# The z columns of the first two sequence tiles, computed row block by row block

## The chip, the cores and the metric

The kernel runs on one core of a Trainium2 chip. A core has TensorE (PE, matrix multiplies), VectorE (DVE), ScalarE (ACT), GpSimd (POOL) and SyncE (SP, which issues most transfers). Each engine works through its own list of instructions in order; semaphores hold an instruction until what it needs is there. The metric is the device time of one execution in microseconds, the median of several runs.

## The reference

One encoder layer: an RMS norm, one projection W_in, attention and a state-space branch on its columns, gates, and an output projection.

```python
h = _rms_norm(x, pre_norm_g[l])
z = h @ w_in[l]
z_q, z_kv, z_kr, g_attn, u_ssm, g_ssm = jnp.split(z, split_points, axis=-1)
attn = _mla_attention(z_q, z_kv, z_kr, positions, ...)
ssm = _s5_bidirectional(u_ssm, ...)
...
x = x + _rms_norm(mixed, post_norm_g[l])
```

x is 2048 x 1024, W_in is 1024 x 1984. The change touches only `h @ w_in`, and of it only the first 448 columns (z_q, z_kv and z_kr, which the kernel calls z) of the first two of 16 sequence tiles.

## The kernel before, in words

The first phase computes h @ W_in. The sequence is cut into 16 tiles of 128 positions, which are taken in pairs. A tile is loaded (`load_x`), scaled by its norm (`norm_x`: squares and their sum on ScalarE, a power on GpSimd, the scaling on VectorE), and turned (`turn`: eight 128x128 transposes on TensorE into PSUM).

Everything is multiplied in three passes, to keep float32 accuracy in a faster number format: an operand is split into a high part, which ScalarE writes, and the rest, which VectorE writes (`split`, lines 194 to 200). hh and hl are the parts of the turned x; wh and wl those of a block of weights. `mm3` (lines 202 to 205) issues the three matmuls high x high, high x low, low x high.

W_in's columns come as four blocks: z (448 columns), u, ga and gs (512 each). Each is loaded and split in 8 row blocks of 128 rows (`load_raw`, `split_w`, `load_w`), once, and stays in SBUF. `gemm` makes the z columns of one tile by 8 times 3 matmuls; `gemm_t` makes 256 columns of u or a gate for a pair of tiles, by 2 groups of 8 times 3 matmuls. `do_z` copies z out of PSUM on ScalarE, takes the squares of its two parts there, lets GpSimd scale them, and stores them. `do_u` and `do_gate` do the like.

The order on each engine is the order in which the program issues the instructions; no scheduler moves them. For the first pair that is: load x0 (in two halves), the first four row blocks of z's weights and x1; scale x0; split blocks 0 and 1; turn x0; split blocks 2, 3 and 4; scale x1; split blocks 5 to 7. Then the generator `blocks` (line 563) gives one step at a time: `do_z` of tile 0, with `turn` of tile 1 put in before its row block 5; then the split of u's weights (`load_w(*BLK[1])`); `do_z` of tile 1; then ga's split, the first half of u, gs's split, the second half, and the four gate steps. From the second pair on the weights are there and only x is loaded.

The raw row blocks lie in two rings: 7 buffers (`s5t`), and 8 (`stg`) for every fourth block; a load waits until its buffer is free. PSUM has 5 buffers for results (`psZ`), 2 for transposes and one (`psK`) that is used much later. Behind the first phase come attention with the state-space branch beside it, and the output projection.

Of the kernel before, what the change touches and what calls it, by code (L numbers as in the profile page):

```python
# [12 lines left out]
F32 = mybir.dt.float32  # L13
# [9 lines left out]
P = 128  # L23
SEQ = 2048
DM = 1024
KD = DM // P
NT = SEQ // P
# [4 lines left out]
NZ = 448  # L32
# [116 lines left out]
def tile_hymba(ctx, tc, x, pos, inv_freq, pre_g, w_in, q_g, w_uqT, w_uqr, kv_g, w_ukT, w_uv, attn_g,  # L149
# [4 lines left out]
    V, A, G, PE, SP = nc.vector, nc.scalar, nc.gpsimd, nc.tensor, nc.sync  # L154
# [14 lines left out]
    ident = con.tile([P, P], F32, tag="ident", name="ident")  # L169
# [9 lines left out]
    def small_consts():  # L179
        SP.dma_start(kvg, kv_g)  # L180
        V.tensor_scalar(kvgs, kvg, SCALE, None, ALU.mult)
        SP.dma_start(qg, q_g)
        V.tensor_scalar(qgs, qg, SCALE, None, ALU.mult)
# [9 lines left out]
    def split(hi, lo, src, scale=None):  # L193

        if scale is None:
            A.activation(hi, src, AF.Copy)
            V.tensor_tensor(lo, src, f32(hi), ALU.subtract)
        else:
            A.activation(hi, src, AF.Copy, scale=scale)
            V.scalar_tensor_tensor(lo, src, scale, f32(hi), ALU.mult, ALU.subtract)  # L200

    def mm3(ps, ahi, alo, bhi, blo, first, last):
        PE.matmul(ps, ahi, bhi, start=first, stop=False)  # L203
        PE.matmul(ps, ahi, blo, start=False, stop=False)  # L204
        PE.matmul(ps, alo, bhi, start=False, stop=last)  # L205
# [16 lines left out]
    def pool(st, name, bufs, **kw):  # L222
        return st.enter_context(tc.tile_pool(name=name, bufs=bufs, reuse_waits="tile", **kw))
# [5 lines left out]
    hh = hp.tile([P, KD, 2, P], F32R, tag="hh", name="hh")  # L229
    hl = hp.tile([P, KD, 2, P], F32R, tag="hl", name="hl")  # L230
# [6 lines left out]
    psZ = pool(ph1, "psZ", 5, space=PSUM)  # L237
    psK = pool(ph1, "psK", 1, space=PSUM)

    BLK = [("z", 0, NZ), ("u", 960, 512), ("ga", 448, 512), ("gs", 1472, 512)]  # L240
    wh, wl = {}, {}

    def load_raw(nm, c0, n, k):
        ring, tag = (stg, "st") if k % 4 == 3 else (s5t, "sc")
        raw = ring.tile([P, 512], F32, tag=tag, name=f"raw_{nm}{k}")
        SP.dma_start(raw[:, :n], w_in[k * P:(k + 1) * P, c0:c0 + n])
        return raw

    def split_w(nm, n, k, raw):
        if nm not in wh:  # L250
            wh[nm] = wp[nm].tile([P, KD, n], F32R, tag=f"wh_{nm}", name=f"wh_{nm}")
            wl[nm] = wp[nm].tile([P, KD, n], F32R, tag=f"wl_{nm}", name=f"wl_{nm}")
        split(wh[nm][:, k, :], wl[nm][:, k, :], raw[:, :n], preg[:, k:k + 1])

    def load_w(nm, c0, n, ks=range(KD)):
        for k in ks:
            split_w(nm, n, k, load_raw(nm, c0, n, k))

    def load_x(s):
        xt = xp.tile([P, DM], F32, tag="xt", name=f"xt{s}")  # L260
        SP.dma_start(xt, xv[s])
        return xt

    def norm_x(xt):
        junk = jp.tile([P, DM], BF16, tag="junk", name="junk")
        ss = sm.tile([P, 1], F32, tag="ss", name="ss")
        A.activation(junk, xt, AF.Square, accum_out=ss)
        r = rsqrt_of(ss, 1, 1.0 / DM)
        V.tensor_scalar(xt, xt, r, None, ALU.mult)

    def turn(xt, t):

        pts = []
        for j in range(2):
            pt = psT.tile([P, 4, P], F32, tag="pt", name="pt")
            for k in range(4):
                PE.transpose(pt[:, k, :], xt[:, (4 * j + k) * P:(4 * j + k + 1) * P], ident)
            pts.append(pt)
        for j in range(2):
            split(hh[:, 4 * j:4 * j + 4, t, :], hl[:, 4 * j:4 * j + 4, t, :], pts[j])  # L280

    def gemm(nm, n, t, between=None):
        ps = psZ.tile([P, 512], F32, tag="z", name=f"z_{nm}")
        for k in range(KD):
            if k == 5 and between:
                between()
            mm3(ps[:, :n], hh[:, k, t, :], hl[:, k, t, :], wh[nm][:, k, :], wl[nm][:, k, :], k == 0, k == KD - 1)
        return ps

    def do_z(s, between=None):  # L290
        ps = gemm("z", NZ, s % 2, between)
        z = stg.tile([P, 512], F32, tag="st", name="zst")
        A.activation(z[:, :NZ], ps[:, :NZ], AF.Copy)
        junk = jp.tile([P, DM], BF16, tag="junk", name="junk")
        ss = sm.tile([P, 2], F32, tag="ss2", name="ss2")
        A.activation(junk[:, :256], z[:, 0:256], AF.Square, accum_out=ss[:, 0:1])
        A.activation(junk[:, 256:384], z[:, 256:384], AF.Square, accum_out=ss[:, 1:2])
        v = sm.tile([P, 2], F32, tag="rv2", name="rv")
        r = sm.tile([P, 2], F32, tag="rr2", name="rr")
        V.tensor_scalar(v[:, 0:1], ss[:, 0:1], 1.0 / 256, EPS, ALU.mult, ALU.add)  # L300
        V.tensor_scalar(v[:, 1:2], ss[:, 1:2], 1.0 / 128, EPS, ALU.mult, ALU.add)
        G.tensor_tensor(r, v, nhalf[:, 0:2], ALU.pow)
        G.tensor_scalar(z[:, 0:256], z[:, 0:256], r[:, 0:1], None, ALU.mult)
        G.tensor_scalar(z[:, 256:384], z[:, 256:384], r[:, 1:2], None, ALU.mult)
        G.dma_start(z_d[s], z[:, :NZ])
# [256 lines left out]
    def step():  # L562

        VM.n -= BUDGET
        while VM.n < 0 and next(gen, "end") != "end":
            pass

    def blocks(s):


        pair = [(do_u, (s, 0)), (do_u, (s, 1)), (do_gate, (s, "ga", 0, 0)), (do_gate, (s, "ga", 1, 2)),
                (do_gate, (s, "gs", 0, 4)), (do_gate, (s, "gs", 1, 6))]
        x1 = xs[1]
        z0, z1 = [(do_z, (s, (lambda: turn(x1, 1)) if s <= 2 else None))], [(do_z, (s + 1,))]
        for f, a in z0 + z1 + pair if s in (0, NT - 2) else z0 + pair + z1:
            f(*a)
            yield

# [25 lines left out]
    xt = xp.tile([P, DM], F32, tag="xt", name="xt0")  # L604
# [1 line left out]
    for c in halves:  # L606
        SP.dma_start(xt[:, c], xv[0][:, c])
    SP.dma_start(preg, pre_g)
    raws = [load_raw(*BLK[0], k) for k in range(4)]
    xs = [xt, load_x(1)]  # L610
    ss = sm.tile([P, 2], F32, tag="ss2", name="ss")
    junk = jp.tile([P, DM], BF16, tag="junk", name="junk")
    for j, c in enumerate(halves):
# [3 lines left out]
    G.tensor_tensor(r, v, nhalf[:, :1], ALU.pow)  # L617
    for c in halves:
        V.tensor_scalar(xt[:, c], xt[:, c], r, math.sqrt(DM), ALU.mult, ALU.mult)
    for k in range(2):  # L620
        split_w("z", NZ, k, raws[k])
    turn(xt, 0)
    for k in range(2, 4):
        split_w("z", NZ, k, raws[k])
    load_w(*BLK[0], range(4, 5))
    norm_x(xs[1])
    load_w(*BLK[0], range(5, KD))
    for s in range(0, NT, 2):
        last = s + 2 == NT
        blk = blocks(s)  # L630
        for n in range(4 if last else 8):
            next(blk)
            if s == 0 and n == 0:
                load_w(*BLK[1])
                small_consts()
            if not last and n == 0:
                xs = [load_x(s + 2), load_x(s + 3)]
            if s == 0 and n in (1, 2):
                load_w(*BLK[1 + n])
            if not last and n in ((4, 5) if s == 0 else (1, 2)):  # L640
                norm_x(xs[n - (4 if s == 0 else 1)])
            if n == 7 and s == 0:
                turn(xs[0], 0)
            elif n >= 6 and s > 0:
                turn(xs[n - 6], n - 6)
            if s > 0:
                step()
# [895 lines left out]
    for t in range(8 * NU + LAG + AVLAG + 2):  # L1543
        n, i = divmod(t, 8)
# [44 lines left out]
        if n < NU and b + 1 < 8:  # L1589
            k = 8 * h + i  # L1590
# [70 lines left out]
def build(nc, arrays):  # L1661
    args = [nc.dram_tensor(f"in_{k}_dram", a.shape, mybir.dt.from_np(a.dtype), kind="ExternalInput").ap()
            for k, a in arrays.items()]
    outs = [nc.dram_tensor(f"out_{i}_dram", shape, mybir.dt.from_np(np.dtype(dtype)), kind="ExternalOutput").ap()
            for i, (shape, dtype) in enumerate(_OUTS)]
    with tile.TileContext(nc) as tc:
        tile_hymba(tc, *args, *outs)
# [11 lines left out]
```

## Time and profile before

| | us |
|---|---|
| median of 3 runs (lowest, highest) | 1382.09 (1381.69, 1382.13) |
| the profiled execution | 1382.02 |
| its span, first to last instruction | 1380.2 |
| TensorE busy | 1344.5 (97% of the span) |
| VectorE, ScalarE, GpSimd busy | 972.8, 796.5, 650.4 |

The profile gives, for each instruction, the engine, its start and how long it took. Busy time of TensorE counts overlapping matmuls once; the distance between the starts of two neighbours is its pace. A name such as `z_z<-wh_z,hh` says what is written and what is read. A row with a count (x8) is a run of like instructions, with the time from the first's start to the last's end.

### The profile page before, as it was taken

Reading aid. Unit: us, or ns where it says so; the run is one execution under the profiler, and the core shown is the slowest. Engines: PE = TensorE matmul, PEld = TensorE weight load, DVE = VectorE, ACT = ScalarE, POOL = GpSimd, SP = SyncE. Lnnn points to the kernel's source line nnn. Section 1 sums busy time; section 2 is a strip of 40 time slices with the busy share of each in tenths; the row PEclk is TensorE's granted clock in tenths of the full one; section 3 lists DMA queues with packets and bytes.
Section 4 is the critical chain, followed back from the end, with each engine's and each line's share of the span. In section 5 each row is a group of like instructions: output and inputs, shape, how many; then the busy total and the mean of one; then the engine's idle time right before and its main releaser. Section 6 shows DMA issues by size and latency. Waiting matters only on the chain.

```text
span 1380.2 us, 24302 instructions
## 1 busy us (share of the span) xinstructions
PE 1344.5 (97%) x9016; PEld 1216.5 (88%) x9016; DVE 972.8 (70%) x1812; ACT 796.5 (58%) x1828; POOL 650.4 (47%) x680
## 2 busy tenths in 40 slices
PE   7999999999989999999999999999999989999998
PEld 7999999999978888898888888888888778888886
DVE  6456564433288878888878879887887895867774
ACT  7312221222248778778777777777787775545542
POOL 2102311322447576575576666756641885333440
PEclk9999999999999999999999999999999999999999
DMA  8322323352630020201202011110101344455332
GB/s 300 89 54 72 88 69 78 87 130 62 147 90 23 9 67 9 51 24 28 47 5 63 13 35 41 27 41 9 30 9 35 100 130 111 146 174 168 124 107 92
DMA packets 122135, 102.93 MB, mean 75 GB/s; under 512 B 14672, under 2 KB 107104, under 8 KB 122016
## 3 DMA queue, kind: packets, MB, share of 16 engines
q1 hardware_dynamic: 110384, 89.43, 23.3%
q0 software_dynamic: 2272, 7.62, 2.2%
q10 hardware_dynamic: 9360, 4.33, 1.6%
q8 instruction: 70, 1.15, 0.4%
q14 instruction: 49, 0.40, 0.1%
HBM read 63.80 MB, written 37.54 MB: 73 GB/s over the span
## 4 chain that ended last, share of the span: by engine, by line
PE 79%; DVE 8%; POOL 5%; issue 3%; ACT 3%; DMA 2%; SPq 1%; POOLq 0%; DVEq 0%; ACTq 0%
PE pt L1151 5%; PE po L203 4%; PE po L204 4%; PE po L205 4%; PE sc L1103 3%; PE sc L1104 3%; PE sc L1107 3%; PE sc L1106 3%; PE av L1172 3%; PE av L1171 3%; PE av L1173 3%; PE sc L1105 3%; PE z_ga L204 2%; PE z_ga L205 2%; PE z_ga L203 2%
## 5 line engine op out<-in xcount | busy, mean ns | idle before, releaser
L1575 DVE TENSOR_TENSOR plo<-pt,phi 128x512 fp32r<-128x512 f32 x255 | 175.4, 688 | 58.0 <-ACT phi L1159 53.6
L1114 ACT ACTIVATE e<-sc,nm 128x512 f32<-128x512 f32 x256 | 175.8, 687 | 69.6 <-DVE nm L1108 69.0
L1108 DVE TENSOR_REDUCE nm<-sc 128x1 f32<-128x512 f32 x256 | 174.3, 681 | 49.1 <-PE sc L1107 47.7
L1159 ACT ACTIVATE phi<-pt 128x512 fp32r<-128x512 f32 x256 | 152.7, 596 | 75.3 <-PE pt L1151 74.2
L1143 ACT ACTIVATE e<-e,f 128x512 f32<-128x512 f32 x226 | 163.8, 725 | 1.5 <-DVE f L1132 1.5
L1171 PE MATMUL av<-phi,kn_h 128*128 128x256 f32 x512 | 163.2, 319 | 0.2 <-ACT avs L1176 0.2
L1151 PEld LDWEIGHTS pt<-ident,e 128*128 128x128 f32 x1024 | 127.1, 141 | 38.2 <-DVE e L1139 4.3
L1151 PE MATMUL pt<-ident,e 128*128 128x128 f32 x1024 | 153.9, 272 | 4.1 <-DVE e L1139 3.4
L1173 PE MATMUL av<-plo,kn_h 128*128 128x256 f32 x512 | 144.5, 282 | 0.4 <-DVE plo L1575 0.4
L1172 PE MATMUL av<-phi,kn_l 128*128 128x256 f32 x512 | 144.3, 282 | 0.0
L1103 PE MATMUL sc<-kT_h,qo 128*128 128x512 f32 x256 | 115.2, 450 | 5.4 <-ACT e L1114 3.5
L1021 POOL TENSOR_TENSOR hc<-G,t 128x512 f32<-128x512 f32 x32 | 42.0, 1312 | 135.9 <-DVE G L1573 99.3
L203 PE MATMUL po<-woh,ah 128*128 128x512 f32 (+1 forms) x264 | 102.5, 388 | 0.0
L204 PE MATMUL po<-wol,ah 128*128 128x512 f32 (+1 forms) x264 | 102.4, 388 | 0.0
L205 PE MATMUL po<-woh,al 128*128 128x512 f32 (+1 forms) x264 | 102.3, 388 | 0.0
L1104 PE MATMUL sc<-kT_l,qo 128*128 128x512 f32 x256 | 101.2, 395 | 0.0
L1107 PE MATMUL sc<-krS,qo 128*128 128x512 f32 x256 | 100.8, 394 | 0.0
L1106 PE MATMUL sc<-krS,qo 128*128 128x512 f32 x256 | 100.8, 394 | 0.0
L1105 PE MATMUL sc<-kT_h,qo 128*128 128x512 f32 x256 | 100.3, 392 | 0.0
L1171 PEld LDWEIGHTS av<-phi,kn_h 128*128 128x128 f32 x512 | 97.3, 190 | 0.5 <-ACT avs L1176 0.4
L1172 PEld LDWEIGHTS av<-phi,kn_l 128*128 128x128 f32 x512 | 97.3, 190 | 0.1
L1173 PEld LDWEIGHTS av<-plo,kn_h 128*128 128x128 f32 x512 | 96.4, 188 | 0.7 <-DVE plo L1575 0.6
(338 smaller groups left out, 4109.4 us busy)
## 6 DMA issues: line engine op xcount, KB each, us to landing
g_d<-gst SPq DMA_DIRECT2D x64, 128.0 KB, 2.0
g<-g_d SPq DMA_DIRECT2D x16, 512.0 KB, 6.1
xr<-in_x_dram SPq DMA_DIRECT2D x16, 512.0 KB, 6.7
xt<-in_x_dram SPq DMA_DIRECT2D x15, 512.0 KB, 3.8
out_dram<-res SPq DMA_DIRECT2D x15, 512.0 KB, 3.1
u_d<-ust ACTq DMA_DIRECT2D x64, 64.0 KB, 2.1
u<-u_d SPq DMA_DIRECT2D x64, 64.0 KB, 2.5
o_d<-o SPq DMA_DIRECT2D x32, 128.0 KB, 1.8
```

The source lines that it names most:

```text
L203: PE.matmul(ps, ahi, bhi, start=first, stop=False)
L204: PE.matmul(ps, ahi, blo, start=False, stop=False)
L205: PE.matmul(ps, alo, bhi, start=False, stop=last)
L1103: PE.matmul(ps, qo[:, 0, w], kT_h[:, c], start=True, stop=False)
L1108: V.tensor_reduce(st["nm"][:, qt, kb:kb + 1], ps, AX.X, ALU.max, negate=True)
L1114: A.activation(e, st.pop("s"), AF.Exp, bias=st["nm"][:, qt, kb:kb + 1], accum_out=st["L"][:, qt, kb:kb + 1])
L1143: A.activation(e, e, AF.Copy, scale=f)
L1151: PE.transpose(pt[:, kk, qt, :], st["e"][qt, kt // 4][:, o:o + P], ident)
L1171: PE.matmul(o, kn_h[:, kt, :], hi[:, w], start=kt == 0, stop=False)
L1172: PE.matmul(o, kn_l[:, kt, :], hi[:, w], start=False, stop=False)
L1173: PE.matmul(o, kn_h[:, kt, :], lo[:, w], start=False, stop=kt == NT - 1)
L1575: V.tensor_tensor(lo[0], lo[1], f32(lo[2]), ALU.subtract)
```

## The change

The z columns of tiles 0 and 1 are no longer made by two calls of `gemm`. Each tile gets its PSUM buffer at once (`pz`), and `rows(k, ...)` issues the three matmuls of row block k for the tiles named. Tile 0 takes blocks 0 to 3 as they are split; then tile 1 is turned and takes blocks 0 to 3; then both take blocks 4 to 7 in turn. Only then does `do_z` follow for both, with the finished PSUM buffer. The load of x1 moves ahead of row blocks 2 and 3; all eight loads of z's weights are issued ahead of the first computation; and 24 transposes of the identity into an unused buffer stand first on TensorE. The steps of the first pair's generator lose the two `do_z`; the splits of u's and ga's weights and the loads of x2 and x3 follow the two `do_z`, ahead of the first u step.

```diff
--- before.py
+++ after.py
@@ -287,8 +287,9 @@
             mm3(ps[:, :n], hh[:, k, t, :], hl[:, k, t, :], wh[nm][:, k, :], wl[nm][:, k, :], k == 0, k == KD - 1)
         return ps
 
-    def do_z(s, between=None):
-        ps = gemm("z", NZ, s % 2, between)
+    def do_z(s, between=None, ps=None):
+        if ps is None:
+            ps = gemm("z", NZ, s % 2, between)
         z = stg.tile([P, 512], F32, tag="st", name="zst")
         A.activation(z[:, :NZ], ps[:, :NZ], AF.Copy)
         junk = jp.tile([P, DM], BF16, tag="junk", name="junk")
@@ -572,7 +573,7 @@
                 (do_gate, (s, "gs", 0, 4)), (do_gate, (s, "gs", 1, 6))]
         x1 = xs[1]
         z0, z1 = [(do_z, (s, (lambda: turn(x1, 1)) if s <= 2 else None))], [(do_z, (s + 1,))]
-        for f, a in z0 + z1 + pair if s in (0, NT - 2) else z0 + pair + z1:
+        for f, a in pair if s == 0 else z0 + z1 + pair if s == NT - 2 else z0 + pair + z1:
             f(*a)
             yield
 
@@ -606,8 +607,13 @@
     for c in halves:
         SP.dma_start(xt[:, c], xv[0][:, c])
     SP.dma_start(preg, pre_g)
-    raws = [load_raw(*BLK[0], k) for k in range(4)]
+    raws = [load_raw(*BLK[0], k) for k in range(2)]
     xs = [xt, load_x(1)]
+    raws += [load_raw(*BLK[0], k) for k in range(2, KD)]
+
+    warm = psK.tile([P, 4, P], F32, tag="k", name="warm")
+    for n in range(24):
+        PE.transpose(warm[:, n % 4, :], ident, ident)
     ss = sm.tile([P, 2], F32, tag="ss2", name="ss")
     junk = jp.tile([P, DM], BF16, tag="junk", name="junk")
     for j, c in enumerate(halves):
@@ -617,26 +623,44 @@
     G.tensor_tensor(r, v, nhalf[:, :1], ALU.pow)
     for c in halves:
         V.tensor_scalar(xt[:, c], xt[:, c], r, math.sqrt(DM), ALU.mult, ALU.mult)
-    for k in range(2):
+    pz = [psZ.tile([P, 512], F32, tag="z", name=f"z_z{t}") for t in range(2)]
+
+    def rows(k, *ts):
+        for t in ts:
+            mm3(pz[t][:, :NZ], hh[:, k, t, :], hl[:, k, t, :], wh["z"][:, k, :], wl["z"][:, k, :], k == 0, k == KD - 1)
+    split_w("z", NZ, 0, raws[0])
+    turn(xt, 0)
+    for k in range(1, 3):
         split_w("z", NZ, k, raws[k])
-    turn(xt, 0)
-    for k in range(2, 4):
-        split_w("z", NZ, k, raws[k])
-    load_w(*BLK[0], range(4, 5))
+        rows(k - 1, 0)
     norm_x(xs[1])
-    load_w(*BLK[0], range(5, KD))
+    split_w("z", NZ, 3, raws[3])
+    rows(2, 0)
+    rows(3, 0)
+    turn(xs[1], 1)
+    split_w("z", NZ, 4, raws[4])
+    for k in range(4):
+        rows(k, 1)
+    for k in range(4, KD):
+        if k + 1 < KD:
+            split_w("z", NZ, k + 1, raws[k + 1])
+        rows(k, 0, 1)
+    for t in range(2):
+        do_z(t, ps=pz[t])
     for s in range(0, NT, 2):
         last = s + 2 == NT
         blk = blocks(s)
-        for n in range(4 if last else 8):
+        if s == 0:
+            load_w(*BLK[1])
+            small_consts()
+            xs = [load_x(2), load_x(3)]
+            load_w(*BLK[2])
+        for n in range(2 if s == 0 else 0, 4 if last else 8):
             next(blk)
-            if s == 0 and n == 0:
-                load_w(*BLK[1])
-                small_consts()
-            if not last and n == 0:
+            if 0 < s < NT - 2 and n == 0:
                 xs = [load_x(s + 2), load_x(s + 3)]
-            if s == 0 and n in (1, 2):
-                load_w(*BLK[1 + n])
+            if s == 0 and n == 2:
+                load_w(*BLK[3])
             if not last and n in ((4, 5) if s == 0 else (1, 2)):
                 norm_x(xs[n - (4 if s == 0 else 1)])
             if n == 7 and s == 0:
```

In the four excerpts below, rows of one engine stand in its order; a number behind a name tells buffers apart. First ScalarE, from the end of z's weights to u's, before. zst is the copy of a tile's z out of PSUM (z_z), the two rows behind it are its squares, and wh_u is the high part of u's weights from row block raw_u.

```order
L293 ACTIVATE zst_238<-z_z_199 128x448
L296 ACTIVATE junk_240,ss2_241<-zst_238 128x256
L297 ACTIVATE junk_240,ss2_241<-zst_238 128x128
L199 ACTIVATE wh_u_254<-raw_u0_252,preg_82 128x512
L199 ACTIVATE wh_u_254<-raw_u1_258,preg_82 128x512
L199 ACTIVATE wh_u_254<-raw_u2_262,preg_82 128x512
L199 ACTIVATE wh_u_254<-raw_u3_266,preg_82 128x512
L199 ACTIVATE wh_u_254<-raw_u4_270,preg_82 128x512
L199 ACTIVATE wh_u_254<-raw_u5_274,preg_82 128x512
L199 ACTIVATE wh_u_254<-raw_u6_278,preg_82 128x512
L199 ACTIVATE wh_u_254<-raw_u7_282,preg_82 128x512
L293 ACTIVATE zst_319<-z_z_294 128x448
```

And ScalarE in the changed kernel, from the last row block of z's weights to the second of u's:

```order
L199 ACTIVATE wh_z_186<-raw_z7_147,preg_82 128x448
L294 ACTIVATE zst_288<-z_z0_184 128x448
L297 ACTIVATE junk_290,ss2_291<-zst_288 128x256
L298 ACTIVATE junk_290,ss2_291<-zst_288 128x128
L294 ACTIVATE zst_302<-z_z1_185 128x448
L297 ACTIVATE junk_304,ss2_305<-zst_302 128x256
L298 ACTIVATE junk_304,ss2_305<-zst_302 128x128
L199 ACTIVATE wh_u_318<-raw_u0_316,preg_82 128x512
L199 ACTIVATE wh_u_318<-raw_u1_322,preg_82 128x512
```

The copy and squares of the second tile, which stood behind all eight row blocks of u, stand ahead of the first. The other two are TensorE around the transposes of the second tile (pt<-ident,xt1), before:

```order
L203 MATMUL z_z_199<-wh_z_151,hh_101 128x448
L204 MATMUL z_z_199<-wl_z_152,hh_101 128x448
L205 MATMUL z_z_199<-wh_z_151,hl_102 128x448
L277 MATMUL pt_215<-ident_71,xt1_139 128x128 x4
L277 MATMUL pt_220<-ident_71,xt1_139 128x128 x4
L203 MATMUL z_z_199<-wh_z_151,hh_101 128x448
L204 MATMUL z_z_199<-wl_z_152,hh_101 128x448
```

And in the changed kernel, where z_z0 and z_z1 are the two tiles:

```order
L203 MATMUL z_z0_184<-wh_z_186,hh_101 128x448
L204 MATMUL z_z0_184<-wl_z_187,hh_101 128x448
L205 MATMUL z_z0_184<-wh_z_186,hl_102 128x448
L277 MATMUL pt_230<-ident_71,xt1_135 128x128 x4
L277 MATMUL pt_235<-ident_71,xt1_135 128x128 x4
L203 MATMUL z_z1_185<-wh_z_186,hh_101 128x448
L204 MATMUL z_z1_185<-wl_z_187,hh_101 128x448
```

Before, the transposes stood behind row block 4 of tile 0, and that tile's block 5 followed. Now they stand behind tile 0's block 3, and tile 1's block 0 follows. On VectorE the split of row block 3, which the matmul with wl_z ahead of the transposes needs, stands behind the scaling of x1; before, x1's scaling stood behind the split of block 4, and blocks 5 to 7 behind it.

## Rows read from the trace of the kernel before

**Rows 1.** The page: busy time of the engines, and TensorE's slices.

```profile
PE 1344.5 (97%) x9016; PEld 1216.5 (88%) x9016; DVE 972.8 (70%) x1812; ACT 796.5 (58%) x1828; POOL 650.4 (47%) x680
...
PE   7999999999989999999999999999999989999998
```

**Rows 2.** Windows: each engine's busy us (count), clock, DMA share, GB/s.

```profile
25.50:57.02 31.52, 31.52 (x266) 31.52 (x265) 14.95 (x23) 14.59 (x25) 5.66 (x6) 1.00 0.49 155
```

**Rows 3.** Timeline, TensorE's opening: start us, us, engine, line, operation, tiles.

```profile
6.50 1.97 PE L277 MATMUL pt<-ident,xt 128*128 128x128 f32 x8 [6.50 <-DVE xt L619]
8.30 0.74 PE L203 MATMUL z_z<-wh_z,hh 128*128 128x448 f32 x1
...
11.15 0.57 PE L204 MATMUL z_z<-wl_z,hh 128*128 128x448 f32 x1
11.52 0.57 PE L205 MATMUL z_z<-wh_z,hl 128*128 128x448 f32 x1
...
12.15 0.37 PE L204 MATMUL z_z<-wl_z,hh 128*128 128x448 f32 x1
...
12.96 0.36 PE L205 MATMUL z_z<-wh_z,hl 128*128 128x448 f32 x1
14.50 1.06 PE L277 MATMUL pt<-ident,xt 128*128 128x128 f32 x8 [1.17 <-DVE xt L269]
...
17.24 0.36 PE L203 MATMUL z_z<-wh_z,hh 128*128 128x448 f32 x1
...
21.94 0.36 PE L205 MATMUL z_z<-wh_z,hl 128*128 128x448 f32 x1
```

**Rows 4.** Timeline, TensorE's u matmuls, the last late one to ga's first.

```profile
25.28 0.38 PE L205 MATMUL z_u<-hh,wl_u 128*128 128x256 f32 x1
25.50 0.28 PE L203 MATMUL z_u<-hh,wh_u 128*128 128x256 f32 x1
...
33.99 0.28 PE L203 MATMUL z_ga<-hh,wh_ga 128*128 128x256 f32 x1
```

**Rows 5.** Timeline, ScalarE's opening.

```profile
11.04 0.67 ACT L199 ACTIVATE wh_z<-raw_z,preg 128x448 fp32r<-128x448 f32 x1 [0.82 <-DMA raw_z<-in_w_in_dram]
11.61 1.04 ACT L267 ACTIVATE junk<-xt 128x1024 bf16<-128x1024 f32 x1
...
15.16 1.09 ACT L196 ACTIVATE hh<-pt 128x512 fp32r<-128x512 f32 x2 [0.74 <-PE pt L277]
17.43 0.55 ACT L293 ACTIVATE zst<-z_z 128x448 f32<-128x448 f32 x1 [1.18 <-PE z_z L205]
...
18.72 5.01 ACT L199 ACTIVATE wh_u<-raw_u,preg 128x512 fp32r<-128x512 f32 x8
```

**Rows 6.** Timeline, VectorE's opening.

```profile
13.60 0.75 DVE L269 TENSOR_SCALAR xt<-xt,rr 128x1024 f32<-128x1024 f32 x1 [0.67 <-POOL rr L190]
14.27 1.87 DVE L200 SCALAR_TENSOR_TENSOR wl_z<-raw_z,preg,wh_z 128x448 fp32r<-128x448 f32 x3
...
19.46 5.76 DVE L200 SCALAR_TENSOR_TENSOR wl_u<-raw_u,preg,wh_u 128x512 fp32r<-128x512 f32 x8 [0.46 <-ACT wh_u L199]
...
29.36 2.13 DVE L200 SCALAR_TENSOR_TENSOR wl_ga<-raw_ga,preg,wh_ga 128x512 fp32r<-128x512 f32 x3 [0.19 <-ACT wh_ga L199]
```

**Rows 7.** Loads of blocks 2 and 3, and of x1: issues, time to landing.

```profile
L246 SPq DMA_DIRECT2D raw_z<-in_w_in_dram x2: 432/432/432, 3.1 to 3.6; - x2
...
DMA to landing us min/median/max: 4.6/4.6/4.7
...
L261 SPq DMA_DIRECT2D xt<-in_x_dram x1: 431/431/431, 4.0 to 4.0; - x1
...
DMA to landing us min/median/max: 6.4/6.4/6.4
```

**Rows 8.** Timeline, the next tile: ScalarE's first half, and the third matmul.

```profile
57.71 1.08 ACT L196 ACTIVATE hh<-pt 128x512 fp32r<-128x512 f32 x2
...
59.19 0.47 PE L205 MATMUL z_z<-wh_z,hl 128*128 128x448 f32 x1 [0.16 <-DVE hl L197]
```

## Prediction

> **What bounds the kernel now.** I read the page first. TensorE is busy 97% of the span and the slices stay at 8 or 9 tenths from the second on, so nearly everything behind the opening is a queue of matmuls, and what delays or advances TensorE in the opening moves the end by as much [rows 1]. The first slice is the one that is not full. The windows say how far the opening reaches: from 25.50 to 57.02 us TensorE has no gap at all, 31.52 busy of 31.52 [rows 2]. So the question is when TensorE, with everything it needs, gets past 25.5.
>
> The timeline of TensorE [rows 3] gives the opening. Eight transposes of tile 0 start at 6.50, when x0 is scaled; the first z matmul starts at 8.30. Two neighbours stand 0.37 apart at 11.15 and 11.52, and last 0.57; from 12.15 one lasts 0.37, and the 23 steps from 17.24 to 21.94 are 0.204 each. That is 448 columns at the lower level (1.2 GHz) and then at the higher (2.4 GHz); the page's clock line does not show the low stretch, the pace does. Tile 1's transposes start at 14.50, tile 1's first z matmul at 17.24, its last at 21.94. The u matmuls follow, and the one at 25.28 is the last that starts late; the 72 behind it, up to the first ga matmul at 33.99, run at 0.118 [rows 4].
>
> What ends last at 25.28 is not TensorE. It is the split of the u weights: ScalarE starts it at 18.72 [rows 5], VectorE does its half from 19.46 to 25.22 without a rest, 8 instructions in 5.76 us [rows 6]. A group of u matmuls needs all eight row blocks. In this kernel most of that split lies beside the 24 matmuls of tile 1 (17.24 to 22.3), because ScalarE's order is: copy and squares of tile 0's z (17.43 to 18.72), then the u weights, and tile 1's z only behind them.
>
> **The change part by part.** *Identity transposes.* 24 transposes of ident, once ident is there. Eight at the lower level take 1.97 us including the 0.47 tail of one, which is 0.21 each, so 24 take 5.1 us; ident is written in the second microsecond, so they end near 6.5, when x0's transposes can start at all [rows 3]. Cost nothing, hidden by x0's loading and scaling; without that cover they would cost what they overrun, some tenths. Their gain would be a faster clock from 6.5 to 12. I put it at nothing too: the matmuls of tile 0 that now stand ahead of tile 1 wait for weights, as the next step shows, and 9 of them at 0.37 would fit as well.
>
> *Second tile loaded sooner.* The load moves ahead of raw blocks 2 and 3. Before, blocks 2 and 3 were issued at 3.08 and 3.55 and took 4.6 and 4.7, so they landed at 7.7 and 8.25; x1 was issued at 4.03 and landed at 10.43, 2.2 us behind block 3 [rows 7]. With the 512 KB ahead of it, block 2 lands at 7.7 + 2.2 = 9.9 and block 3 near 10.4. No DMA is added; the blocks behind see the same bytes ahead as before. But ScalarE has block 2 ahead of x1's squares, so they start at 9.9 + 0.65 = 10.55 instead of 11.61 [rows 5], 1.05 sooner, and x1 is scaled at 13.3 instead of 13.60 + 0.75 = 14.35 [rows 6].
>
> TensorE cannot use that: in its order the three matmuls of block 3 stand ahead of tile 1's transposes, and VectorE splits block 3 only behind the scaling of x1. That split takes 0.63 (three took 1.87) and ends at 13.95; two more matmuls, 0.41, and the transposes start at 14.4, against 14.50 [rows 3]. So the sooner load is worth 0.1 us there. Bounds: if block 2 still landed at 7.7, the squares could start 2.2 sooner and the transposes at 12.2; if x1 and the blocks shared the queues so that block 2 came as late as block 4 did (used at 11.04 [rows 5]), the squares would keep their 11.6 and the transposes come 1.05 later, at 15.5. I take 14.4, since block 3 landed 2.2 ahead of x1 and the bytes only change places.
>
> *z by row blocks.* Before, 15 matmuls of tile 0 stood ahead of tile 1's transposes and 9 + 24 behind; now 12 ahead and 12 + 24 behind, three more, 0.6 us. The 9 matmuls of tile 0 also used to start 0.8 us behind the start of the transposes; now tile 1's own matmuls come first, and wait for its split: 0.66 from the transposes to ScalarE's first half (14.50 to 15.16), and 1.48 from there to the third matmul, which needs VectorE's half, taken from the next tile (57.71 to 59.19) [rows 5, 8]. So the third starts at 14.4 + 0.66 + 1.48 = 16.54, the other 33 follow at 0.204, and the last z matmul starts at 23.3 instead of 21.94. Blocks 4 to 7 are split by 19.5 and hold nothing up.
>
> *Both tiles end together.* This is the term that decides. Tile 0 used to be done at 17.4, with all 24 matmuls of tile 1 still to come. Now it ends three matmuls before tile 1. Its copy to SBUF, which waits for that, stood 0.19 behind the start of the next matmul (17.24 and 17.43) [rows 3, 5], so it starts at 22.67 + 0.2 + 0.19 = 23.06. Behind that waiting copy on ScalarE stand its squares, then the copy and squares of tile 1, and only then the u weights; each tile's set takes 18.72 - 17.43 = 1.29 [rows 5]. So the first u block starts at 23.06 + 2 x 1.29 = 25.64, not 18.72: 6.92 later. Nothing of TensorE lies beside the split any more. TensorE waits some 2.7 us for the first block and then for each block in turn. The last late u matmul moves from 25.28 to 32.2, and the 72 behind it and all that follows keep their pace.
>
> ga and gs weights shift along with u, since their splits stand behind it on ScalarE and VectorE; before, ga was split by 31.5 [rows 6] and used from 33.99, and now ga's split no longer has tile 1's set in front of it. GpSimd's two scalings stand close together now, but nothing waits for their z. SP's other loads keep their order.
>
> The sum: +6.9 us on the profiled execution of 1382.02 (its span of 1380.2 and 1.8 around it; the median of the runs shown is 1382.09), so 1388.9, or 0.5%. With the bounds on the transposes the plain case is 1386.7 to 1390.0.
>
> **The clock, and a rule that speaks against the new transposes.** In rows 3 the pace changes between 11.52 and 12.15, 3.4 to 3.8 us after the first z matmul and over 5 after the first transpose; that does not tell which of the two counted. The Trainium skill, "TensorE: Matmul & The Clock Gate", section "Part 4: PE-mode transpose", holds that a transpose does not count as a busy TensorE for the clock in the way that a matmul does. By that rule the 24 transposes would raise nothing; by the other reading the clock is up before 8 us. For the plain sum both give 1388.9, since tile 0's matmuls wait for weights; where they differ is the second rival below.
>
> **The rivals.** *First, not slower.* All z work runs without a wait from 6.50 on: with two turns of 1.06 and 47 steps of 0.204 the last z matmul starts at 18.2, tile 0's copy 0.24 before it (as 23.06 to 23.3 above) at 18.0, and the first u block 2.58 later at 20.5 instead of 18.72. The loss is 1.8 us: 1383.8, no measurable change. For this x1 would have to be scaled by 10.0 us (the first turn and 12 matmuls behind 6.50), where the sum has 13.3. It shows how far faster is: the last z matmul would have to start by 16.4, sooner than TensorE can do the work. I give 5% to this and 2% to anything faster.
>
> *Second, the clock is low when the dense z matmuls start at 16.5*, because twelve scattered matmuls and transposes did not raise it or did not hold it. Before, it took 3.6 us of matmuls from 8.30 to raise it [rows 3]; at 0.37 instead of 0.204 such a stretch loses 1.6 us, and the u split comes later by as much: 1390.5. For it: between 9 and 14 us TensorE now has 12 matmuls, 2.5 us of work, where it had 15 in one run. Against it: the wait from 13.3 (12.96 and the 0.36 of its matmul) to 14.50 left the pace high. By the rule of the Trainium skill above it would be likelier. From the rows I give it 22%.
>
> *Third, the clock falls in the new wait before u*, 2.7 us of nothing and then 0.35 of every 0.72. While the weights are late that costs nothing (three low matmuls of 256 columns fit in 0.72), but the dense ones behind 32.2 would lose up to 1.6 as above: 1390.5. No wait before is as long, so the rows do not decide. 13%.
>
> *That the change does not do what it says* is in the plain case already: the second tile is loaded sooner and scaled sooner, and TensorE gets to it at the old time.
>
> **How the numbers follow.** Plain case 58%, the two clock cases 35%, not slower 7%. The predicted time is the plain one, 1388.9. The range, 1386.7 to 1391.6, holds the plain case with its bounds and either clock case with 1.1 more. A measurement of this kernel tells 0.2%, 2.8 us, from no change: slower by more than that 93%, within it 5%, faster 2%.
>
> **What would show it.** Right: tile 1's transposes near 14.4; the last z matmul near 23.3; wh_u's first instruction near 25.6, right behind two copies and their squares; TensorE waiting for wh_u and wl_u of every row block; the first ga matmul near 40.9 against 33.99, and the same shift at every later mark. Wrong: wh_u starting before 22, or ga's first matmul before 37, or a later wait that shrinks by several microseconds and takes the shift up.

## The result and the profile after

The changed kernel takes 1390.24 us (median of 6 runs, 1386.75 to 1392.47) against 1382.11 (6 runs of the kernel before beside it): ratio 1.0059, 95% interval 1.0047 to 1.0072. It is slower by 8.1 us; 1388.9 was forecast, with a range of 1386.7 to 1391.6. The profiled execution took 1392.17, one of the longer of the six and 0.6 above the range, with a span of 1390.4. Its marks are compared below with those of the profiled execution of before (1382.02).

The page of the kernel after shows the same picture as [rows 1], busy time by engine and TensorE's slices:

```profile
PE 1355.4 (97%) x9040; PEld 1222.8 (88%) x9040; DVE 972.7 (70%) x1812; ACT 797.0 (57%) x1828; POOL 653.2 (47%) x680
...
PE   7999999999989999999999999999999989999998
```

TensorE has 24 instructions more, and 10.9 us more of busy time. Neither says where the time went: 5.1 us of it are identity transposes beside loads, and the slices do not differ at all.

The timeline of TensorE after, as in [rows 3]:

```profile
1.37 5.14 PE L616 MATMUL warm<-ident 128*128 128x128 f32 x24 [1.37 <-POOL nhalf L172]
6.46 1.09 PE L277 MATMUL pt<-ident,xt 128*128 128x128 f32 x8
7.80 0.47 PE L203 MATMUL z_z<-wh_z,hh 128*128 128x448 f32 x1 [0.25 <-ACT hh L196]
...
9.72 0.47 PE L204 MATMUL z_z<-wl_z,hh 128*128 128x448 f32 x1 [0.40 <-DVE wl_z L200]
...
11.19 0.47 PE L203 MATMUL z_z<-wh_z,hh 128*128 128x448 f32 x1 [0.80 <-ACT wh_z L199]
11.91 0.47 PE L204 MATMUL z_z<-wl_z,hh 128*128 128x448 f32 x1 [0.25 <-DVE wl_z L200]
...
12.79 0.61 PE L203 MATMUL z_z<-wh_z,hh 128*128 128x448 f32 x1 [0.20 <-ACT wh_z L199]
14.43 0.74 PE L204 MATMUL z_z<-wl_z,hh 128*128 128x448 f32 x1 [1.03 <-DVE wl_z L200]
14.97 0.57 PE L205 MATMUL z_z<-wh_z,hl 128*128 128x448 f32 x1
15.34 1.91 PE L277 MATMUL pt<-ident,xt 128*128 128x128 f32 x8
...
18.00 0.57 PE L205 MATMUL z_z<-wh_z,hl 128*128 128x448 f32 x1
...
25.56 0.36 PE L205 MATMUL z_z<-wh_z,hl 128*128 128x448 f32 x1
```

The first z matmul starts 0.5 sooner than before (7.80 against 8.30), tile 1's transposes 0.84 later (15.34 against 14.50), the last z matmul 3.6 later (25.56 against 21.94). The eight transposes of tile 0 last 1.09 where they lasted 1.97, and those of tile 1 last 1.91 where they lasted 1.06: the clock was up early and went down again. The windows of the kernel after give it (us of the window, busy us and count by engine, granted clock, DMA share, GB/s):

```profile
6.20:12.90 6.70, 4.75 (x21) 2.50 (x19) 3.98 (x8) 4.45 (x8) 0.46 (x1) 1.00 0.93 326
13.00:19.70 6.70, 5.67 (x18) 4.44 (x18) 3.82 (x6) 3.01 (x6) 0.00 (x0) 0.50 0.33 124
19.90:30.00 10.10, 7.08 (x35) 5.90 (x33) 3.07 (x8) 4.81 (x15) 2.76 (x3) 1.00 0.65 209
30.10:33.40 3.30, 3.19 (x14) 3.19 (x15) 3.30 (x7) 3.30 (x6) 3.12 (x3) 0.50 0.83 260
```

The granted clock is 0.50, the lower level, in two stretches: where tile 1 is turned and begun, and in most of the u matmuls that wait for weights. Before 12.9, when TensorE was busy for 4.75 of 6.70 us with waits between nearly all groups, it was 1.00; the dense z matmuls behind 18 brought it back.

ScalarE after, as in [rows 5], and VectorE, as in [rows 6]:

```profile
10.46 0.67 ACT L199 ACTIVATE wh_z<-raw_z,preg 128x448 fp32r<-128x448 f32 x1 [1.67 <-DMA raw_z<-in_w_in_dram]
11.04 1.04 ACT L267 ACTIVATE junk<-xt 128x1024 bf16<-128x1024 f32 x1
...
16.44 0.60 ACT L196 ACTIVATE hh<-pt 128x512 fp32r<-128x512 f32 x1 [3.70 <-PE pt L277]
...
25.35 0.55 ACT L294 ACTIVATE zst<-z_z 128x448 f32<-128x448 f32 x1 [5.23 <-PE z_z L205]
...
26.63 0.52 ACT L294 ACTIVATE zst<-z_z 128x448 f32<-128x448 f32 x1
...
27.89 5.00 ACT L199 ACTIVATE wh_u<-raw_u,preg 128x512 fp32r<-128x512 f32 x8
```

```profile
13.03 0.75 DVE L269 TENSOR_SCALAR xt<-xt,rr 128x1024 f32<-128x1024 f32 x1 [0.67 <-POOL rr L190]
...
28.63 5.64 DVE L200 SCALAR_TENSOR_TENSOR wl_u<-raw_u,preg,wh_u 128x512 fp32r<-128x512 f32 x8 [0.46 <-ACT wh_u L199]
```

ScalarE stands idle for 5.23 us in front of tile 0's copy, does two sets of 1.28 and 1.26, and begins the u weights at 27.89 instead of 18.72. The u matmuls after, as in [rows 4], the first, the last late one, and ga's first:

```profile
28.65 0.38 PE L203 MATMUL z_u<-hh,wh_u 128*128 128x256 f32 x1 [2.73 <-ACT wh_u L199]
...
34.33 0.39 PE L205 MATMUL z_u<-hh,wl_u 128*128 128x256 f32 x1 [0.18 <-DVE wl_u L200]
...
42.96 0.28 PE L203 MATMUL z_ga<-hh,wh_ga 128*128 128x256 f32 x1
```

TensorE waits 2.73 for the first u block and a little for some of the others. ga's first matmul is 8.97 later than before, and there the shift stays: the next tile's first half on ScalarE and its third matmul [rows 8] come at 66.68 and 68.16, 8.97 later each, and TensorE's matmuls keep that distance to the end of the first phase.

```profile
66.68 1.08 ACT L196 ACTIVATE hh<-pt 128x512 fp32r<-128x512 f32 x2
```

The last matmul of the whole kernel starts 10.18 later in these two executions (1373.24 and 1383.42). The 1.2 us more came late, in short waits of TensorE in attention: the matmul that starts at 403.12 before starts at 412.34 now (9.22 later), that of 1081.74 at 1090.26 (8.52), that of 1104.88 at 1114.65 (9.77). Whether they come in every run is not known; the median of all runs is 8.1 later, not 10.

Loads after, as in [rows 7]: block 2 by itself, and x1.

```profile
L246 SPq DMA_DIRECT2D raw_z<-in_w_in_dram x1: 432/432/432, 3.6 to 3.6; - x1
...
DMA to landing us min/median/max: 6.9/6.9/6.9
...
L261 SPq DMA_DIRECT2D xt<-in_x_dram x1: 432/432/432, 3.1 to 3.1; - x1
DMA to landing us min/median/max: 6.8/6.8/6.8
```

x1 is issued 0.9 sooner and lands 0.5 sooner (9.9 against 10.43). Block 2, issued at 3.6 instead of 3.08, lands at 10.5 instead of 7.7.

### The profile page after: what moved, and what is told of

Its sections match the earlier page's. It is cut to its first block, busy times and chain, and to the rows that moved or that the text cites. A ratio compares the mean times of both kernels' runs of the same rounds, so it can differ in the third digit from the quotient of the medians.

```text
span 1390.4 us, 24349 instructions
## 1 busy us (share of the span) xinstructions
PE 1355.4 (97%) x9040; PEld 1222.8 (88%) x9040; DVE 972.7 (70%) x1812; ACT 797.0 (57%) x1828; POOL 653.2 (47%) x680
## 4 chain that ended last, share of the span: by engine, by line
PE 77%; DVE 9%; POOL 5%; issue 3%; ACT 3%; DMA 2%; SPq 1%; POOLq 0%; DVEq 0%; ACTq 0%
PE pt L1175 5%; PE po L203 4%; PE po L204 4%; PE po L205 4%; PE sc L1127 3%; PE sc L1128 3%; PE sc L1131 3%; PE sc L1130 3%; PE av L1196 3%; PE av L1197 3%; PE av L1195 3%; PE sc L1129 3%; PE z_ga L204 2%; PE z_ga L205 2%; PE z_ga L203 2%
```

## The experiments

The theory was that the order of ScalarE's work decides: both tiles' copies and squares stand ahead of the u weights, and wait for z matmuls that now end together. The rivals were the clock and the loads. The kernel before took 1382.16 (16 runs) beside the first four kernels of the table and 1381.63 (17 runs) beside the last four; each ratio is to the runs beside it.

| kernel | median us (lowest to highest, runs) | ratio to before, 95% | ga's first matmul (before 33.99) |
|---|---|---|---|
| e1_u_first | 1386.0 (1383.84 to 1387.53, 6) | 1.0027 [1.0016, 1.0039] | 36.20 |
| e2_no_warm | 1390.96 (1390.68 to 1393.03, 5) | 1.0068 [1.0055, 1.0081] | 42.29 |
| e3_x1_late | 1389.3 (1387.75 to 1391.46, 5) | 1.0052 [1.004, 1.0065] | 40.16 |
| e4_warm_only | 1381.88 (1380.57 to 1385.49, 11) | 1.0002 [0.9993, 1.0011] | 35.54 |
| e5_filled | 1389.77 (1388.94 to 1390.58, 5) | 1.0055 [1.0042, 1.0068] | 41.53 |
| e6_u_between | 1389.23 (1387.69 to 1393.04, 6) | 1.0058 [1.0046, 1.0071] | 42.09 |
| e7_mixed | 1383.63 (1382.51 to 1385.93, 11) | 1.0015 [1.0007, 1.0024] | 33.32 |
| e8_before_u_behind | 1387.68 (1386.9 to 1391.31, 5) | 1.0047 [1.0035, 1.0059] | 39.03 |

**The u weights ahead of both copies.** The kernel after, with one line moved:

```diff
         rows(k, 0, 1)
+    load_w(*BLK[1])
     for t in range(2):
         do_z(t, ps=pz[t])
...
         if s == 0:
-            load_w(*BLK[1])
             small_consts()
```

> The changed kernel with one move: ScalarE and VectorE split the u weights ahead of the two z copies instead of behind them. Theory (the order of the copies decides): the u split no longer waits for the end of z; it starts right behind the last z block, near 20.1 us in a profile like the one of the changed kernel, and ends near 26.2. TensorE goes from z to u without its 2.7 us wait, the first ga matmul comes between 34.5 and 37 instead of 42.96, and the time is 1382.5 to 1385. Rival (the loss lies in the z phase itself, in the transposes of tile 1 and the low clock there): z still ends near 25.6, only the clock's second fall goes, and the time is 1388 or more.

ScalarE in its opening, and ga's first matmul:

```profile
20.08 5.24 ACT L199 ACTIVATE wh_u<-raw_u,preg 128x512 fp32r<-128x512 f32 x8
25.23 0.52 ACT L294 ACTIVATE zst<-z_z 128x448 f32<-128x448 f32 x1
```

```profile
36.20 0.28 PE L203 MATMUL z_ga<-hh,wh_ga 128*128 128x256 f32 x1
```

The u weights are split mostly beside the z matmuls (20.08 to 26.34, with VectorE's half), the first u matmul comes at 25.00 with no wait, and 4.2 of the 8.1 us return. The median, 1386.0, is 1.0 above what was expected. What is left in the opening, 2.2 us, is z itself: its last matmul starts at 24.79 and not at 21.94, in part since the clock was low here too (0.62 on the mean from 13.00 to 19.70). Another 1.9 us of its profiled execution came behind the opening.

**The reverse, in the kernel before.** u's split, and with it the small constants and the loads of x2 and x3, go behind tile 1's z. Nothing else of the change is in it.

```diff
-            if s == 0 and n == 0:
+            if s == 0 and n == 1:
                 load_w(*BLK[1])
                 small_consts()
-            if not last and n == 0:
+            if not last and n == (1 if s == 0 else 0):
                 xs = [load_x(s + 2), load_x(s + 3)]
```

> The kernel before with one thing of the change: both z copies, with their squares, stand ahead of the u split on ScalarE. Nothing else moves; no identity transposes, x1 at its old place. Theory (the order of the copies decides): z ends at 22.3 as before, the second copy starts there, the u split starts near 23.6 instead of 18.72, the last late u matmul moves by 4.9 us, and the time is 1386.5 to 1388.7 (the upper end if the clock falls while TensorE waits for u). Rival (the u split has slack that hides it): 1382 to 1383.

Its ScalarE and its TensorE (tile 1's copy, the u weights, and the u matmuls up to ga):

```profile
22.45 0.54 ACT L293 ACTIVATE zst<-z_z 128x448 f32<-128x448 f32 x1 [3.52 <-PE z_z L205]
23.73 5.00 ACT L199 ACTIVATE wh_u<-raw_u,preg 128x512 fp32r<-128x512 f32 x8
```

```profile
24.49 0.39 PE L203 MATMUL z_u<-hh,wh_u 128*128 128x256 f32 x1 [2.08 <-ACT wh_u L199]
...
39.03 0.28 PE L203 MATMUL z_ga<-hh,wh_ga 128*128 128x256 f32 x1
```

The order by itself, with z made as before (its last matmul at 22.05), costs 5.04 us up to ga and 6.05 on the median: most of the change's loss. Tile 0's copy is out of the way early here, so one set stands in front of the u weights and not two.

**One set less.** The kernel after, with u's split between the two copies:

```diff
-    for t in range(2):
-        do_z(t, ps=pz[t])
+    do_z(0, ps=pz[0])
+    load_w(*BLK[1])
+    do_z(1, ps=pz[1])
```

> The changed kernel with the split of the u weights moved ahead of tile 1's z copy, so that only tile 0's copy and squares stand ahead of it. Theory (each tile's set costs its 1.29 us, and the larger part is that the first set waits for the end of z): 1.3 us less than the changed kernel, 1388 to 1389.5. Rival (the second set is the loss, and the first is as harmless as before): 4 us less, near 1386, as with u ahead of both.

Its ScalarE:

```profile
25.34 0.54 ACT L294 ACTIVATE zst<-z_z 128x448 f32<-128x448 f32 x1 [5.52 <-PE z_z L205]
26.63 5.00 ACT L199 ACTIVATE wh_u<-raw_u,preg 128x512 fp32r<-128x512 f32 x8
```

The u weights start 1.26 sooner than in the kernel after, one set, and ga's first matmul 0.87 sooner. The median falls by 1.0, but the kernel before was 0.5 faster beside it, and the intervals of the two ratios overlap nearly whole: the profile shows the 0.87, the times do not.

**The clock held up.** The kernel after, with identity transposes into the unused buffer in TensorE's waits: 8, 6 and 14 in z, 22 ahead of u, two behind each of the eight row blocks of u's first group.

```diff
+    gaps = [2] * KD
+
+    def fill(m):
+        for n in range(m):
+            PE.transpose(warm[:, n % 4, :], ident, ident)
...
+        fill(8 * (k - 1))
         rows(k - 1, 0)
+    fill(6)
     norm_x(xs[1])
...
     rows(2, 0)
+    fill(14)
     rows(3, 0)
...
+    fill(22)
     for t in range(2):
         do_z(t, ps=pz[t])
```

> The changed kernel with more identity transposes in TensorE's waits: 8 and 6 between tile 0's early row blocks, 14 ahead of block 3, 22 between z and u, and 2 behind each row block of the first u group. They keep TensorE busy, and the order of everything else stays. Theory (the clock's two falls are what the changed kernel loses beyond the plain sum): the clock stays high from about 6 us on, tile 1's transposes start near 14.4, the last z matmul near 23.0, the first ga matmul near 40.5, and the time is 1388.0 to 1389.2 with less spread than the 5.7 us of the changed kernel. Rival (the falls cost nothing, since weights are what is late): 1390 or more, as the changed kernel.

Two of the windows of the kernel after, in this one:

```profile
13.00:19.70 6.70, 6.28 (x38) 5.12 (x37) 4.71 (x8) 3.31 (x6) 0.12 (x1) 1.00 0.38 128
...
30.10:33.40 3.30, 3.30 (x26) 3.05 (x26) 3.30 (x8) 3.10 (x5) 2.95 (x3) 1.00 0.92 327
```

And the last z matmul:

```profile
23.89 0.36 PE L205 MATMUL z_z<-wh_z,hl 128*128 128x448 f32 x1
```

The clock is 1.00 where it was 0.50. The last z matmul starts at 23.89 instead of 25.56: the low stretch in z had cost 1.67 us. The second low stretch had cost nothing, for from the end of u's split to ga's first matmul it is 8.69 in the kernel after (42.96 less 34.27) and 8.77 before (33.99 less 25.22). In the opening ga gains 1.43, to 41.53, where 40.5 was expected. The time does not show it: the median falls by 0.5, the kernel before was as much faster beside it, and 1389.77 lies between what the theory and the rival expected.

**x1's load back at its place.** The kernel after, with x1 behind raw blocks 2 and 3:

```diff
-    raws = [load_raw(*BLK[0], k) for k in range(2)]
+    raws = [load_raw(*BLK[0], k) for k in range(4)]
     xs = [xt, load_x(1)]
-    raws += [load_raw(*BLK[0], k) for k in range(2, KD)]
+    raws += [load_raw(*BLK[0], k) for k in range(4, KD)]
```

> The changed kernel with x1's load back behind raw blocks 2 and 3. Theory (the sooner load only trades places with blocks 2 and 3): blocks 2 and 3 are split 2 us sooner, x1 lands near 10.4, its squares start near 10.5 as now, its transposes start within 0.5 us of the changed kernel's 15.34, and the time is within 1 us of the changed kernel's. Rival (the sooner load is worth its 1 us): 1 us slower or more, transposes later than 16.

Its ScalarE, and TensorE's turn of tile 1 and last z matmul:

```profile
10.02 1.06 ACT L267 ACTIVATE junk<-xt 128x1024 bf16<-128x1024 f32 x1 [0.59 <-DMA xt<-in_x_dram]
```

```profile
13.94 1.03 PE L277 MATMUL pt<-ident,xt 128*128 128x128 f32 x8
...
22.76 0.36 PE L205 MATMUL z_z<-wh_z,hl 128*128 128x448 f32 x1
```

Loaded later, x1 is squared 1.02 sooner (10.02 against 11.04), and tile 1 is turned 1.4 sooner: ScalarE has block 2 ahead of the squares, and block 2 is what the moved load delays. Tile 1's turn was expected within 0.5 us of 15.34, so the load did more here than trade places. In this profile the clock never falls in z, and ga comes 2.8 sooner. On the median it is 0.9, which the intervals do not separate. So the sooner load gains nothing; whether it costs is not settled.

**The identity transposes, taken out and alone.** The kernel after without the 24, and the kernel before with them:

```diff
-    warm = psK.tile([P, 4, P], F32, tag="k", name="warm")
-    for n in range(24):
-        PE.transpose(warm[:, n % 4, :], ident, ident)
```

> The changed kernel without the 24 identity transposes. Theory (tile 0's matmuls wait for weights, so the clock ahead of 13 us buys nothing): the same time as the changed kernel within 1.5 us, near 1390, and TensorE's pace is low from 6.5 us until some time between 16 and 21. Rival (the early clock is worth something, since the transposes do raise it): 1 to 3 us slower than the changed kernel.

> The kernel before with the 24 identity transposes in front and nothing else. Theory (they raise the clock near 6 us, but tile 0 then waits for weights and tile 1's transposes start at 14.5 as before): 1381.7 to 1382.7. Rival one (the matmuls of tile 0, faster, leave gaps in which the clock falls, as in the changed kernel at 12.96): up to 1.6 us slower. Rival two (they are a gain by themselves): 1381 or less.

Windows of before with the transposes:

```profile
2.00:4.80 2.80, 2.80 (x15) 2.80 (x14) 0.00 (x0) 1.28 (x5) 0.00 (x0) 1.00 0.88 242
...
15.20:18.50 3.30, 3.30 (x12) 3.00 (x11) 2.20 (x4) 1.20 (x2) 0.00 (x0) 0.50 0.85 237
```

And from its timeline of TensorE, two stretches of the transposes:

```profile
1.64 2.98 PE L614 MATMUL warm<-ident 128*128 128x128 f32 x13
...
4.84 1.07 PE L614 MATMUL warm<-ident 128*128 128x128 f32 x8
```

Without them the kernel after takes 1390.96 against 1390.24, and before with them 1381.88 against 1382.16: no gain or cost shows. They do raise the clock. Thirteen take 2.98 us, some 0.21 from start to start, and the last eight 1.07, some 0.11, with no matmul of the kernel issued yet. (The clock column says 1.00 from 2.00 to 4.80; as in before, it does not show the low stretch at the start, and the pace does.) But in this profile the clock fell again at tile 1, so that run's last z matmul came 1.63 late; its time, 1385.11, is one of the two highest of the eleven.

**A mix without the waits.** x1 at its old place, all loads of z up front, identity transposes in TensorE's waits, tile 0 through block 6 before u's split, and u's split ahead of both copies:

```diff
-    for k in range(1, 3):
+    for k in range(1, 4):
         split_w("z", NZ, k, raws[k])
         rows(k - 1, 0)
+        fill(3)
     norm_x(xs[1])
...
+    for k in range(4, 7):
+        split_w("z", NZ, k, raws[k])
     turn(xs[1], 1)
-    split_w("z", NZ, 4, raws[4])
-    for k in range(4):
+    for k in range(4, 7):
+        rows(k, 0)
+    split_w("z", NZ, 7, raws[7])
+    load_w(*BLK[1])
+    for k in range(7):
         rows(k, 1)
-    for k in range(4, KD):
-        if k + 1 < KD:
-            split_w("z", NZ, k + 1, raws[k + 1])
-        rows(k, 0, 1)
+    rows(7, 0, 1)
...
         if s == 0:
-            load_w(*BLK[1])
```

> A version meant to beat both: x1 loaded where the kernel before has it, all z weights loaded at once, identity transposes in front and in TensorE's waits, tile 0's row blocks 0 to 3 while x1 is on its way, blocks 4 to 6 behind tile 1's transposes, and the u split ahead of both z copies. Theory: transposes of tile 1 near 13.5, the last z matmul near 21.5, u dense from there, the first ga matmul near 33.0, 1 us ahead of before: 1380.7 to 1381.9. Rival (TensorE has the same work left once x1 is there, and the u split ends as late as before): 1382 to 1383, no gain.

ga's first matmul, and two matmuls of TensorE after the first phase:

```profile
33.32 0.28 PE L203 MATMUL z_ga<-hh,wh_ga 128*128 128x256 f32 x1
...
399.66 0.39 PE L203 MATMUL psr<-wqr_h,zh 128*128 128x256 f32 x1 [1.12 <-DVE zl L749]
...
404.75 0.50 PE L1131 MATMUL sc<-kT_h,qo 128*128 128x512 f32 x1 [0.26 <-ACT e L1142]
```

The same two before, and the clock between them in this kernel:

```profile
399.39 0.39 PE L203 MATMUL psr<-wqr_h,zh 128*128 128x256 f32 x1 [0.82 <-DVE zl L721]
...
403.12 0.50 PE L1103 MATMUL sc<-kT_h,qo 128*128 128x512 f32 x1 [0.44 <-ACT e L1114]
```

```profile
400.30:403.50 3.20, 3.20 (x11) 2.61 (x11) 1.26 (x4) 0.78 (x2) 0.34 (x1) 0.51 0.00 0
```

The opening is 0.67 shorter than before, and the kernel is still 2.0 us slower on the median, outside both expectations. In its profile TensorE keeps the 0.67 to the end of the first phase. It then loses 0.9 on balance in waits for what the other engines make (0.27 behind at 399.66) and 1.36 more up to 404.75, where the clock is at its lower level; that stretch had no low clock before. Why the clock falls there, and whether it does in the other runs, stays open. All eleven runs are slower than the median of before, and no version tried beats the kernel before.

## Why the prediction was right

*The order on ScalarE* was the term that decides, and it is shown from both sides: put into the kernel before it costs 6.05, taken out of the kernel after it returns 4.2. The two sets were forecast at 1.29 each and took 1.28 and 1.26; TensorE's wait for the first u block at 2.7, and took 2.73; the pace of the rest at that of before, and from the last late u matmul to ga's first it is 8.63 (42.96 less 34.33) against 8.71.

*The number was nearer than the working.* The median is 1.3 above 1388.9, but the profiled execution, the only one against which the steps can be held, is 3.3 above it and outside the range: the opening was 2.1 longer than the sum had it, and 1.2 more came behind it. That the median came nearer is in part luck, since the shorter executions had less of this for reasons that no run shows.

*The plain sum was too small, by 2.1 us in the opening:* ga at 42.96, not 40.9. All of it lies ahead of the last z matmul, 25.56 and not 23.3, in three steps.

- Loads, 0.5. Block 2 was to land at 9.9 and the squares to start at 10.55; it landed at 10.5 and they started at 11.04. The step added to block 2 the 2.2 us by which x1 had landed behind block 3. In fact x1 took 6.8 where it had taken 6.4, block 2 6.9 instead of 4.6, as loads would that share the queues. The bound in which they share the queues was named and not taken; what came lies about halfway to it.
- The two matmuls of block 3 ahead of the turn, 0.5: 0.91 (14.43 to 15.34) and not 0.41, at the low clock.
- Tile 1's z, 1.3: the third matmul 2.66 behind the turn's start and not 2.14, and the other 33 in 7.56 and not 6.73, until the clock came back.

The last two are the second rival, that the clock is low when the dense z matmuls start. It was given 22% and priced at 1.6; it came true in the profile of the kernel after, and measured 1.67 there by the kernel that holds the clock. What happened in that opening is the plain case with that rival on top, and its 1390.5 is nearer to the median than 1388.9. In time the rival is not shown: with the clock held the loss against the kernel before beside it is 8.1 us as well, and ga still comes 0.6 later than the plain sum had it (41.53 and not 40.9). What holding it did change is the spread of the runs, 5.7 to 1.6. The mean granted clock of each run is known, 0.994 to 0.997 in the six of the kernel after and 0.997 to 0.999 in the runs of before, so the clock was low for longer in each of the six than in most runs of before; where in the kernel it was low is known for the profiled one alone. The argument against the rival, that a wait from 13.3 to 14.50 had left the pace high before, weighed one wait; now five waits, of 0.20 to 1.03 us, stood between the matmuls from 7.80 to 14.43.

The rule weighed there does not hold for this kernel's transposes (`PE.transpose`; the trace lists them as MATMUL): the Trainium skill, "TensorE: Matmul & The Clock Gate", section "Part 4: PE-mode transpose", has it that a transpose does not count as a busy TensorE for the clock in the way that a matmul does. Eight transposes of tile 0, with nothing but transposes ahead of them, took 1.09 instead of 1.97, and the measurement decides.

*The third rival*, the clock falling in the wait before u, came true as an event (0.50 from 30.10 to 33.40) and cost nothing: TensorE was at most 0.2 us behind the weights and waited again for the last of them (0.18 at 34.33), which was the cover named.

*The first rival*, z without a wait, could not happen, since x1 was scaled by 13.78 and not by 10.0. *Identity transposes at nothing*: no difference shows, either way. *The sooner load at 0.1* was not seen as a gain at all.

The opening does not give the whole time to better than some microseconds. In the profile of every one of the nine kernels the execution grew by more than ga's first matmul was late, by 0.3 (e6_u_between) to 3.6 us (e7_mixed); the forecast had nothing for that. None of it comes in the first phase, where TensorE keeps its distance to before in all nine. It comes behind that phase, in attention above all, and all nine lose some (0.2 to 2.9 us) where the kernel before has its marks from 1070 to 1106; since it is one execution of before that all are held against, part of that may be its own good luck. The rest is open.

## What to carry to other kernels

When two tiles are interleaved they end together, and whatever stands behind both results on the list of the engine that copies the results out of PSUM (here ScalarE) then waits for the last: put the next weights' split ahead of those copies, or let one tile end early. A load that is moved forward can cost the ones behind it more than it gains (here 2.8 us for 0.5), and it helps only if its user on the engine does not stand behind one of those. When a dense run of matmuls is broken up to wait for weights, price the low clock for it too; here it cost 1.67 us of the opening in the profile, and nothing that the times could show.

## What the runs showed of the hardware

Transposes of an identity alone doubled TensorE's pace (0.21 to 0.11 us each), yet the clock was given back when the work behind them was full of waits: 0.50 from 13.00 to 19.70. Low stretches also came far from the opening, once each in the profiles of seven of these kernels and not in those of before, of the kernel after and of e1_u_first: between 400 and 420 us in four of them, at 837, 844 and 1090 in the others. Of the kernel with u behind z:

```profile
413.00:416.20 3.20, 3.20 (x11) 2.57 (x11) 1.32 (x3) 1.05 (x3) 1.61 (x3) 0.50 0.07 15
```

TensorE was busy for all of it. What such a stretch costs can be read in two profiles: 1.36 us in e7_mixed (400.30 to 403.50), and in e4_warm_only a matmul ahead of it stands 2.23 later than before (834.88 and 837.11) and one behind it 3.74 (837.30 and 841.04), with the clock at 0.50 from 838.00 to 841.00. So these stretches hold part of what the openings do not explain, but not all: the kernel after and e1_u_first have none, and lost 1.2 and 1.9 us behind their openings. What starts them no run tested.
